# Where the slots lie in SBUF: twelve slots longer by 128 bytes, or three longer by 512

## The chip, the core and the metric

The kernel runs on one core of one Trainium2 chip. The metric is the device time of one launch in microseconds (us). Engines are named as in the profile: PE (TensorE, the matmuls), PEld (its weight loads), DVE (VectorE), ACT (ScalarE), POOL (GpSimd) and SP (SyncE, which issues the DMAs).

## The reference

A decoder block on x of 2048 x 1024 in float32. x is RMS-normed and multiplied by a 1024 x 7680 matrix; the product is cut into a GLU pair, a convolution gate, q, k, v, an attention gate and two merge gates. One branch is a causal depthwise convolution of 31 taps, layer norm, SiLU, gate and a 1024 x 1024 product; the other is attention over a window of 128 with rotary positions and a sink per head (16 query heads, 4 key heads of 64), gate and a 1024 x 1024 product.

```python
glu_in, conv_gate, q, k, v, attn_gate, merge_logits = split(rmsnorm(x, norm_g) @ w_in)
c = silu(layernorm(depthwise_conv(a * sigmoid(b))))        # glu_in = a, b
y_conv = (c * silu(conv_gate)) @ w_conv_out
y_attn = (attention(rope(q), rope(k), v, sinks) * silu(attn_gate)) @ w_attn_out
x = x + (sigmoid(m_conv) * y_conv + sigmoid(m_attn) * y_attn) @ w_out
return rmsnorm(x, final_norm_g)
```

## The kernel before, in words

The 2048 rows are worked in two sweeps of T = 1024, each sweep in two halves of 512 columns. Every large product is made in split precision: each operand is a high part and a remainder, and each block of 128 x 128 x 512 takes three matmuls, high x high, high x remainder, remainder x high (L280). `project` (L267) makes one item: for each half, 8 steps of the inner dimension with 3 matmuls, so 24 matmuls into one PSUM bank, and 48 for both halves. A sweep has 60 items that read the normed input hT (16 for the GLU, 12 for q, k and v, 32 for the gates), then 8 of the attention output (`mm_ya`, moving tiles aT), 8 of the convolution output (`mm_yc`, moving tiles uT) and the last product (L885), which is 16 blocks of 24 with the tiles wo moving and the merged activations mT as weights. Between the matmuls of the items lie those of the attention (from L554: scores `sc` L572 of 256 columns, transposes `tpp` L602, the product with v `ov` L622) and other transposes (`tpf` L361, `tpx` L327, `tpv` L502). The order on PE is written out by hand by the class `Line`, which has planned durations; it depends on no address. DVE carries the convolution (L396).

The weights of an item come through the pool `stage`: raw, high and remainder, 4 buffers of 2048 bytes a partition each, every one holding four weight matrices of 512 bytes a partition. Everything else that is large lives in 43 slots (L75 to L90): 16 named H, 16 A, 8 C and 3 X. A slot holds 1024 floats, 4096 bytes a partition; a matmul's moving operand is either half of it (high part or remainder, 2048 bytes). Slots listed in `WIDE` (all C, a14, a15, h14, h15) are 1056 floats, 4224 bytes, because a GLU tile has 30 more columns ahead of it (L415); GLU tiles only ever use c6, c7 and a14 (L379).

A pool's tiles lie one after another in the order in which their names are first used. The tiles of `const` end at byte 9024 of a partition, the slots follow, then `stage` at 186688 and `work` at 211264. Byte 9024 is 17 x 512 + 320. Since a plain slot is 8 x 512 bytes and a wide one 8 x 512 + 128, the place of a tile within 512 bytes (its remainder, below) changes behind each wide slot. Worked out from the order of use:

| tiles | remainder mod 512 |
|---|---|
| all weight buffers of `stage` | 320 |
| A0 to A5, A7 to A12, H0 to H7, C0, C6, C7 | 320 |
| H8 to H14, C1, A14 | 448 |
| H15, C2, C4 | 64 |
| A6, A13, A15, X0 to X2, C3, C5 | 192 |
| the identity for transposes (`const`) | 128 |

By address, H0 to H7 and the A tiles but A6, A13, A14 and A15 start below 87000, C0 to C3 from 90944 to 103616, H8 to H15 from 112064 to 140864, and the weights lie above 194880.

The moving tiles by item: in the first sweep hT and uT are H0 to H7 for half 0 and H8 to H15 for half 1, aT is A0 to A7 and A8 to A15. In the second, hT and uT are H8 to H15 and then A0 to A7, aT is H0 to H7 and A8 to A15. mT lies where aT lay, wo in C0 to C7 (L846). The v tiles vt are in the first four A (H in the second sweep), vd in X0 to X2 and A15; probabilities pt and pc in A7 to A10 (H7, A8 to A10 in the second sweep).

Of the kernel before, what the change touches and what calls it, by code (L numbers as in the profile page):

```python
# [12 lines left out]
F32 = mybir.dt.float32  # L13
# [6 lines left out]
P = 128  # L20
# [3 lines left out]
T = 1024  # L24
# [4 lines left out]
HALO = TAPS - 1  # L29
# [24 lines left out]
def hybrid_block(ctx: ExitStack, tc: tile.TileContext, x, par_d, w_in, w_conv, sinks, w_attn, w_out,  # L54
# [4 lines left out]
    const = ctx.enter_context(tc.tile_pool(name="const", bufs=1))  # L59
# [16 lines left out]
    A = [f"a{i}" for i in range(16)]  # L76
    C = [f"c{i}" for i in range(8)]
    X = [f"x{i}" for i in range(3)]
    WIDE = set(C) | {"a14", "a15", "h14", "h15"}

    def slot(tag, shape, dt, name):
        n = int(np.prod(shape[1:]))
        full = HALO + T + 2 if tag in WIDE else 1024
        t = slots.tile([P, full], dt, tag=tag, name=name)
        v = t[:, 0:n]
        if len(shape) == 3:
            v = v.rearrange("p (a b) -> p a b", b=shape[2])
        elif len(shape) == 4:
            v = v.rearrange("p (a b c) -> p a b c", b=shape[2], c=shape[3])
        return v  # L90
# [11 lines left out]
    def load_first(half):  # L102
        xs = []
        for j in range(4):
            r0 = (4 * half + j) * P
            xs.append(slot(A[7 * half + j], [P, D], F32, f"xf{half}_{j}"))
            nc.sync.dma_start(out=xs[-1], in_=x2[r0:r0 + P, :])
        return xs
# [4 lines left out]
    ident_r = const.tile([P, P], F32R, name="ident_r")  # L113
    ident = f(ident_r)
    ident_0 = slot(A[4], [P, P], F32, "ident_0")
    make_identity(nc, ident_0)
    dve.tensor_copy(out=ident_r, in_=ident_0)
    ones_0 = slot(A[5], [P, P], F32, "ones_0")
    dve.memset(ones_0, 1.0 / D)
    ones = const.tile([P, P], F32R, name="ones")  # L120
# [39 lines left out]

    d_a = dram.tile([NSWEEP * KC, P, 2, T], F32, name="d_a")
    v_halo = const.tile([P, NKV, 2, HD], F32R, name="v_halo")
    v_last = const.tile([P, 2, P], F32, name="v_last")
    dve.memset(v_last, 0.0)


# [798 lines left out]
```

## Time and profile before

| | |
|---|---|
| median of 3 runs | 2053.18 us (2053.03 to 2053.26) |
| the profiled execution, its own time | 2053.2 us |
| its span, first to last instruction | 2051.5 us |
| granted TensorE clock | 0.999 |
| busy PE, DVE, ACT, POOL | 99%, 65%, 50%, 20% of the span |
| DMA, mean share of 16 engines | 53.3%, 173 GB/s |

So 1.7 us lie outside the span. A matmul's recorded duration covers its way through the array and overlaps the next one's, and its end is modelled; what a matmul costs in a stream is the step from its start to the next one's start. The chain view (work that ended last, in order of time) gives a piece as start, length and count: length by count is the mean step. The timeline gives starts.

### The profile page before, as it was taken

How to read it: one execution, taken by the hardware profiler on the slowest of the kernel's cores; microseconds unless marked ns; L12 is line 12 of the kernel's file. 1: busy time of each engine (PE TensorE's matmuls, PEld its weight loads, DVE VectorE, ACT ScalarE, POOL GpSimd, SP SyncE). 2: the span in 40 equal slices, each digit the busy share in tenths (PEclk: the TensorE clock that was granted, in tenths of full speed). 3: DMA queues.
4: the chain of work that ended last, by engine and by line, in shares of the span. 5: the costliest groups of instructions: out<-in, count | busy, mean ns of one | idle time of the engine just before them, and what ended most of it. 6: DMA issues, size and time to landing. Idle time of an engine off the chain costs nothing.

```text
span 2051.5 us, 27562 instructions
## 1 busy us (share of the span) xinstructions
PE 2031.3 (99%) x9256; PEld 1669.1 (81%) x9256; DVE 1327.4 (65%) x1965; ACT 1027.8 (50%) x2313; POOL 403.4 (20%) x336
## 2 busy tenths in 40 slices
PE   7999999999999999999999999999999999999998
PEld 6888888888888888888888888888888888888886
DVE  4968769988994355123668678689888924441323
ACT  6312477777777463123433125767677764621222
POOL 2335332333323223241001120111011100001200
PEclk9999999999999999999999999999999999999999
DMA  7445655555566757444344555555555577564422
GB/s 249 144 144 167 208 170 160 166 168 172 161 188 212 252 174 244 143 157 169 131 144 138 164 178 188 160 175 174 173 156 171 179 222 257 172 228 138 153 110 82
DMA packets 265821, 355.91 MB, mean 173 GB/s; under 512 B 28112, under 2 KB 126544, under 8 KB 265680
## 3 DMA queue, kind: packets, MB, share of 16 engines
q1 hardware_dynamic: 265680, 354.16, 53.3%
q8 instruction: 73, 1.20, 0.2%
q14 instruction: 68, 0.56, 0.1%
HBM read 234.51 MB, written 119.54 MB: 173 GB/s over the span
## 4 chain that ended last, share of the span: by engine, by line
PE 96%; DVE 2%; DMA 1%; issue 0%; SPq 0%; POOL 0%; ACT 0%; DVEq 0%; POOLq 0%
PE mm_cg L281 9%; PE o L885 9%; PE mm_ma L281 9%; PE mm_ga L281 9%; PE mm_mc L281 9%; PE mm_yc L281 9%; PE mm_ya L281 9%; PE mm_gb L281 8%; PE mm_ag L281 7%; PE mm_q_a L281 4%; PE mm_q_b L281 4%; PE sc L572 3%; PE ov L622 3%; PE mm_v L281 2%; DVE acc L396 2%; PE tpp L602 1%
## 5 line engine op out<-in xcount | busy, mean ns | idle before, releaser
L396 DVE SCALAR_TENSOR_TENSOR acc<-glu,par,acc 128x1024 f32<-128x1024 f32 x464 | 596.3, 1285 | 6.2
L885 PE MATMUL o<-wo,mT 128*128 128x512 f32 x768 | 181.3, 395 | 0.0
L885 PEld LDWEIGHTS o<-wo,mT 128*128 128x128 f32 x768 | 143.2, 188 | 32.0
L281 PE MATMUL mm_cg<-hT,whi_cg 128*128 128x512 f32 x512 | 161.1, 396 | 0.0
L281 PE MATMUL mm_ga<-hT,whi_ga 128*128 128x512 f32 x512 | 160.9, 395 | 0.2 <-ACT whi_ga L253 0.2
L281 PE MATMUL mm_ma<-hT,whi_ma 128*128 128x512 f32 x512 | 161.0, 396 | 0.0
L281 PE MATMUL mm_ag<-hT,whi_ag 128*128 128x512 f32 x512 | 160.8, 395 | 0.0
L281 PE MATMUL mm_gb<-hT,whi_gb 128*128 128x512 f32 x512 | 160.7, 395 | 0.0
L281 PE MATMUL mm_mc<-hT,whi_mc 128*128 128x512 f32 x512 | 159.7, 393 | 0.0
L281 PE MATMUL mm_yc<-uT,whi_yc 128*128 128x512 f32 x512 | 159.5, 393 | 0.0
L281 PE MATMUL mm_ya<-aT,whi_ya 128*128 128x512 f32 x512 | 158.7, 391 | 0.0
L613 POOL TENSOR_SCALAR_AFFINE_SELECT pc<-pt 128x1024 fp32r<-128x1024 f32 x60 | 65.6, 1094 | 428.7 <-DVE pt L242 428.6
L281 PEld LDWEIGHTS mm_yc<-uT,whi_yc 128*128 128x128 f32 x512 | 96.2, 188 | 21.8
L281 PEld LDWEIGHTS mm_mc<-hT,whi_mc 128*128 128x128 f32 x512 | 96.1, 188 | 21.7
L281 PEld LDWEIGHTS mm_ya<-aT,whi_ya 128*128 128x128 f32 x512 | 96.1, 188 | 20.9
L281 PEld LDWEIGHTS mm_ga<-hT,whi_ga 128*128 128x128 f32 x512 | 94.6, 188 | 20.4 <-ACT whi_ga L253 0.6
L281 PEld LDWEIGHTS mm_gb<-hT,whi_gb 128*128 128x128 f32 x512 | 94.7, 188 | 19.9
L281 PEld LDWEIGHTS mm_ag<-hT,whi_ag 128*128 128x128 f32 x512 | 94.3, 188 | 19.4
L281 PEld LDWEIGHTS mm_cg<-hT,whi_cg 128*128 128x128 f32 x512 | 94.2, 188 | 19.5
L281 PEld LDWEIGHTS mm_ma<-hT,whi_ma 128*128 128x128 f32 x512 | 94.2, 188 | 19.3
L592 ACT ACTIVATE ss<-ss,st 128x128 f32<-128x128 f32 x256 | 99.7, 391 | 11.2 <-DVE st L587 10.7
L281 PE MATMUL mm_ga<-hT,wlo_ga 128*128 128x512 f32 x256 | 100.8, 394 | 0.7 <-POOL wlo_ga L242 0.7
(364 smaller groups left out, 4259.3 us busy)
## 6 DMA issues: line engine op xcount, KB each, us to landing
qk<-d_q SPq DMA_DIRECT2D x256, 64.0 KB, 2.2
d_a<-ss SPq DMA_DIRECT2D x128, 128.0 KB, 1.9
aT<-d_a SPq DMA_DIRECT2D x32, 512.0 KB, 5.5
qk<-d_k SPq DMA_DIRECT2D x240, 64.0 KB, 2.0
raw_gb<-in_w_in_dram SPq DMA_DIRECT2D x34, 256.0 KB, 3.2
raw_ga<-in_w_in_dram SPq DMA_DIRECT2D x34, 256.0 KB, 3.3
raw_ag<-in_w_in_dram SPq DMA_DIRECT2D x32, 256.0 KB, 3.7
d_ag<-ag SPq DMA_DIRECT2D x32, 256.0 KB, 2.2
```

What stands on the lines that cost most here:

```text
L281: pe.matmul(out=ps, lhsT=a, rhs=b, start=(k == 0 and i == 0), stop=(k == KC - 1 and i == 2))
L396: dve.scalar_tensor_tensor(out=to, in0=glu[c][:, j:j + T], scalar=tap(c, j), in1=acc[c], op0=ALU.mult, op1=ALU.add)
L572: pe.matmul(out=o, lhsT=q[:, h, :], rhs=r, start=(j == 0), stop=(j == 1))
L592: act.activation(out=sb[:, h, :], in_=sb[:, h, :], func=AF.Exp, scale=SCALE, bias=ngm[:, h:h + 1], accum_out=den[:, h:h + 1])
L602: pe.transpose(out=tpp[:, h, :], in_=sb[:, h, :], identity=ident)
L613: pool.affine_select(out=pc, in_=f(pt), pattern=[[0, 2], [0, GQ], [1, P]], compare_op=ALU.is_ge, fill=0.0, base=0, channel_multiplier=-1)
L622: pe.matmul(out=ov, lhsT=vv, rhs=pp[:, i % 2], start=(i == 0), stop=(i == nm - 1))
L885: pe.matmul(out=ps, lhsT=a[:, c0:c0 + P], rhs=r, start=(k == 0 and i == 0), stop=(k == KC - 1 and i == 2))
```

## The change

```diff
-    WIDE = set(C) | {"a14", "a15", "h14", "h15"}
+    WIDE = {"c6", "c7", "a14"}
...
-        full = HALO + T + 2 if tag in WIDE else 1024
+        full = 1024 + P if tag in WIDE else 1024
...
-    v_last = const.tile([P, 2, P], F32, name="v_last")
+    v_last = const.tile([P, 2 * P + 48], F32, name="v_last")[:, 0:2 * P].rearrange("p (a b) -> p a b", b=P)
```

Twelve slots were 128 bytes longer than the rest; now three are, by 512. Both add up to 1536 bytes, so the slots take as much as before. `v_last` is the last tile of `const` and grows by 48 floats, 192 bytes, of which nothing is used: the slots start at 9216 = 18 x 512, `stage` at 186880 = 365 x 512. With slots of 8 x 512 or 9 x 512 bytes and buffers of 4 x 512, every slot, every weight buffer and every weight matrix in it has the remainder 0. The identity keeps its 128. The tiles of 512 floats in `work`, which hold no operand of the large products, go from 384 to 64. No instruction is added, removed or moved, and no shape changes.

## The prediction

> **What bounds the kernel now.** The page comes first: who is busy, and what the chain that ended last is made of.
>
> ```profile
> span 2051.5 us, 27562 instructions
> PE 2031.3 (99%) x9256; PEld 1669.1 (81%) x9256; DVE 1327.4 (65%) x1965; ACT 1027.8 (50%) x2313; POOL 403.4 (20%) x336
> PE 96%; DVE 2%; DMA 1%; issue 0%; SPq 0%; POOL 0%; ACT 0%; DVEq 0%; POOLq 0%
> ```
>
> PE is the chain. The view of waits, for PE alone, says how much of the span it stood still:
>
> ```profile
> PE tpf L361 <- DVE ident_r L117: 8.4, 1, 8.4
> PE tpf L361 <- DVE xf L354: 2.4, 2, 1.5
> PE sc L572 <- DVE pt L242: 1.0, 1, 1.0
> ```
>
> The two longest are the start, before there is anything to multiply; the third is the longest wait after it, 1.0 us. So the time is the sum of PE's steps, and the question is whether a step depends on where its operands lie. The chain view of two neighbouring blocks of one `mm_yc` item of the first sweep, in which nothing is put between the matmuls, answers it:
>
> ```profile
> 874.48 5.45 PE mm_yc L281 x24
> ...
> 879.93 5.59 PE mm_yc L281 x24
> ```
>
> Same instruction, same shape, same weights (remainder 320); the first block's moving tiles are H0 to H7 (320), the second's H8 to H15 (448, the last 64). The second takes 0.14 us longer, in each of the eight items of this stage. The timeline of the first, where the moving tile is H2 and later, and of the second:
>
> ```profile
> 875.92 0.62 PE L281 MATMUL mm_yc<-uT,whi_yc 128*128 128x512 f32 x2
> ...
> 880.00 0.62 PE L281 MATMUL mm_yc<-uT,whi_yc 128*128 128x512 f32 x2
> ...
> 885.59 0.40 PE L281 MATMUL mm_yc<-uT,whi_yc 128*128 128x512 f32 x1
> ```
>
> From 875.92 to 880.00 are 18 matmuls: 4.08 / 18 = 0.2267 us a step. I call this the settled step: moving operand and weights have the same remainder, and it holds without scatter. The first 6 of that block, still 320 by 320, took 5.45 - 4.08 = 1.37, some 0.228 each: they come right behind a block that did not match, and the stream needs a few matmuls to settle. From 880.00 to 885.59 are 24 steps of 0.2329, and these never settle.
>
> Where the two sweeps swap their tiles, the slow half swaps too (H8 to H15 are half 1 in the first sweep and half 0 in the second), so it goes with the tile and not with the half.
>
> **The change part by part.** All moving tiles and all weights of the large products get the remainder 0, so all of them match. The sum takes every step of theirs at 0.2267. No row shows a pair at remainder 0 itself. I take 0.2267, because it is the only steady value of a matching pair, and matching is what 320 by 320 and 0 by 0 share; the step is bounded above by the 0.2329 of blocks that never settle (the bound below follows where its row stands).
>
> The items and last stages, from the chain view (the first two rows are of a window of the first sweep, the others of the whole span):
>
> ```profile
> 103.14 11.03 PE mm_q_b L281 x48
> 114.16 11.04 PE mm_gb L281 x48
> ...
> 764.63 87.99 PE mm_ya L281 x384
> 852.62 88.33 PE mm_yc L281 x384
> 1069.97 11.07 PE mm_kb L281 x48
> 1127.13 11.07 PE mm_gb L281 x48
> 1171.43 11.07 PE mm_q_a L281 x48
> 1779.53 87.67 PE mm_ya L281 x384
> 1867.19 88.57 PE mm_yc L281 x384
> 1955.77 88.72 PE o L885 x384
> ```
>
> An item of 48 settled steps takes 48 x 0.2267 = 10.88. In the first sweep that saves some 0.155 (11.03 and 11.04), in the second 0.19 (11.07). With 60 such items a sweep: 9.3 + 11.4 = 20.7 us.
>
> A stage of 384 settled steps takes 87.05. That saves 0.94 and 0.62 in the two `mm_ya`, 1.28 and 1.52 in the two `mm_yc`, and 1.67 in the last product; the first sweep's last product is cut up by transposes, and I give it the same 1.67. Together 7.7 us.
>
> The attention has small work between the items. One attention step in the chain view:
>
> ```profile
> 570.60 0.44 PE tpp L602 x4
> 571.03 2.78 PE mm_ma L281 x12
> 573.81 0.94 PE ov L622 x4
> ...
> 575.44 0.95 PE sc L572 x8
> ```
>
> `ov` takes 0.94 for four 512-column steps, of which two have weights at 192; settled it is 0.91, so 0.03 in each of 60 steps (the first step of a key head in the first sweep has no vd): 2.0 us. The scores read q and k from one tile, so they match before and after, and I take no gain; if they came down from 0.119 a step to half of 0.2267, it would be 0.0055 x 8 x 64 = 2.8 us.
>
> Against this stands what goes on unsettling the stream: the identity of the transposes keeps its remainder 128, and the scores are short. The timeline behind one group of scores, in 320 by 320 tiles:
>
> ```profile
> 659.16 1.11 PE L572 MATMUL sc<-qk 128*128 128x256 f32 x8
> 660.11 0.63 PE L281 MATMUL mm_ma<-hT,whi_ma 128*128 128x512 f32 x2
> ...
> 661.49 0.62 PE L281 MATMUL mm_ma<-hT,whi_ma 128*128 128x512 f32 x2
> 661.94 0.39 PE L281 MATMUL mm_ma<-hT,wlo_ma 128*128 128x512 f32 x1
> ```
>
> Six steps from 660.11 to 661.49 take 1.38, against 1.36 settled: 0.02. (The next two, 661.49 to 661.94, take 0.225 each, the shortest pair that these rows show: the bound below for a step at remainder 0.) Behind transposes the chain above has 12 steps in 2.78, against 2.72 settled: 0.06, high rather than low, since half of them read tiles at 448. The counts:
>
> ```profile
> L572 PE MATMUL sc<-qk 128*128 128x256 f32 x480 | 67.1, 282 | 1.0 <-DVE pt L242 1.0
> L602 PE MATMUL tpp<-ident_r,ss 128*128 128x128 f32 x256 | 38.3, 272 | 0.0
> L327 PE MATMUL tpx<-ident_r,x 128*128 128x128 f32 x64 | 9.6, 272 | 0.0
> L502 PE MATMUL tpv<-ident_r,vs 128*128 128x128 f32 x32 | 4.8, 272 | 0.0
> ```
>
> That is 352 / 4 = 88 groups of transposes and some 64 of scores, 88 x 0.06 + 64 x 0.02 = 6.6 us in a stream that matches everywhere. Half of them fall into matching blocks today and cost this already; the other half is new, 3.3 us.
>
> Sum: 20.7 + 7.7 + 2.0 - 3.3 = 27.1 us. The profiled execution took 2053.2 (the median is 2053.18), so about 2026.
>
> The rest I cost at nothing. The start, 8.4 + 2.4 us of waits, hangs on the identity and on x, no large product. A faster PE asks for its inputs sooner, and DVE is the engine with least room, in the table of windows (busy us of PE, PEld, DVE, ACT and POOL in 50 us):
>
> ```profile
> 300.00:350.00 50.00, 50.00 (x239) 41.46 (x238) 48.59 (x66) 35.53 (x89) 13.08 (x12) 1.00 0.51 162
> ```
>
> If that were the bound wherever attention and convolution share DVE in the first sweep, some 300 us, the 1.3% won there, 4 us, would come back as waits of `sc` on `pt`. I leave it to the range. The forecast's own range is 2020 (no new unsettling, and the gain on the scores: 20.7 + 7.7 + 2.0 + 2.8 = 33) to 2039 (a match helps only where nothing is put between: 7.7 and some 20 items a sweep at 0.17, so 14.5).
>
> **The rivals.** First, that the pair at remainder 0 doesn't settle, because 320 is a good place and equality not the reason. Then every step costs 0.2329: items take 11.18, so 60 x 0.145 + 60 x 0.11 = 15.3 more, and the six stages 89.4, so 6.6 more: 22 us slower, 2075. It turns from gain to loss where fewer than about four steps in ten settle, (232.9 - 230.3) / (232.9 - 226.7), with 11.05 / 48 = 0.2303 as the mean now. For it speaks one place in the last product, where a tile at 192 meets weights at 192:
>
> ```profile
> 2036.85 0.70 PE o L885 x3
> ```
>
> 0.233 a step. But these three stand behind tiles at 64 and 192 over weights at 320, and three are too few to settle. Against it: at 320 the tiles of A and of H settle alike, wherever in the lower half of the slots they lie, and with all eight buffers of weights. Chance 0.11.
>
> Second, no change, 2053: the slow tiles are slow for another reason that the change leaves, such as lying high in SBUF, where H8 to H15 remain. For it: H8 to H15 lie above 112000. Against it: in the last product half of the moving tiles, C0 to C3, start below 104000, and at 88.72 / 384 = 0.231 it is the slowest of the tail stages; and the weights lie at the top always. Chance 0.06. The Trainium skill, "TensorE: Matmul & The Clock Gate", step-by-step section of Part 2, would come out here too: it gives PE two independent read ports, so that loading the next weights takes nothing from the running matmul. The two blocks of one item above, 5.45 against 5.59, speak against that as the whole story.
>
> Third, more than forecast: at 512-byte boundaries the settled step is shorter than at 320, down to the 0.225 above. Another 8064 x 0.0017 = 14 us, 2012. Chance 0.05. The Trainium skill, on the same page under "Wait — 56ns, not 53.3ns?", measures 215.7 ns for a warm stream of 512 columns; by that figure the time would be near 1938 as an estimate, and no step of this trace that lasts comes near it.
>
> **How the numbers follow.** The forecast has 0.78. The range leaves out the slower rival (0.11), the deeper gain and a little of the forecast's tails, and takes in no change: 2016 to 2054; the forecast alone has 2020 to 2039. Two parts in a thousand, 4 us, is what a measurement of this kernel can tell from no change: faster 0.78 + 0.05 = 0.83, same 0.06, slower 0.11.
>
> **What would show it.** In the chain view both blocks of an item take 5.44, an undisturbed item 10.88 to 10.9, `mm_ya`, `mm_yc` and the last product 87.0 to 87.3 each. DVE, ACT and DMA groups keep their durations, and PE's waits stay those of the start. If items take 11.18, the first rival holds; if one half of an item still takes 0.14 more than the other, the second; blocks under 5.43, the third. If blocks take 5.44 but the span is not 20 us shorter, the difference must stand as waits of PE on DVE between 300 and 620.

## The result, and the profile after

The changed kernel takes 2028.53 us (2028.24 to 2029.28, 4 runs) against 2053.18 (2053.03 to 2053.26, 4 runs): 24.65 us less, a ratio of 0.9881 with a 95% interval of 0.9863 to 0.9898. The profiled execution took 2029.28, its span is 2027.6.

The first lines of the page, after:

```profile
span 2027.6 us, 27562 instructions
PE 2006.5 (99%) x9256; PEld 1667.3 (82%) x9256; DVE 1324.5 (65%) x1965; ACT 1026.0 (51%) x2313; POOL 403.3 (20%) x336
PE 96%; DVE 2%; DMA 1%; issue 0%; SPq 0%; POOL 0%; ACT 0%; DVEq 0%; POOLq 0%
```

The instructions are the same, and so is the make-up of the chain. PE's busy time fell by 24.8 us, DVE's by 2.9, ACT's by 1.8, POOL's by 0.1. The chain view says where; the columns are start, length, what, and how many:

```profile
57.17 10.88 PE mm_kb L281 x48
...
102.67 10.88 PE mm_q_b L281 x48
113.56 10.88 PE mm_gb L281 x48
...
757.48 87.04 PE mm_ya L281 x384
844.52 87.04 PE mm_yc L281 x384
931.56 19.04 PE o L885 x84
...
1759.43 87.04 PE mm_ya L281 x384
1846.47 87.04 PE mm_yc L281 x384
1933.51 87.05 PE o L885 x384
```

Where before every stage had its own length (87.67 to 88.72), now each is 87.04 or 87.05, and an undisturbed item is 10.88: 0.2267 us a step, in all of them. What is left above that lies around the small work, in the same place of the first sweep that the prediction showed:

```profile
565.44 0.44 PE tpp L602 x4
565.88 2.78 PE mm_ma L281 x12
568.66 0.91 PE ov L622 x4
...
570.25 0.95 PE sc L572 x8
```

The 12 steps behind the transposes still take 2.78, `ov` came from 0.94 to 0.91, and the scores kept their 0.95. The view of waits, for PE:

```profile
PE tpf L361 <- DVE ident_r L117: 8.4, 1, 8.4
PE tpf L361 <- DVE xf L354: 2.7, 2, 1.8
PE sc L572 <- DVE pt L242: 1.3, 1, 1.3
PE tpf L361 <- DVE hT L364: 0.8, 1, 0.8
```

The same waits, the last three longer by 0.3 each; the last of them was, before:

```profile
PE tpf L361 <- DVE hT L364: 0.5, 1, 0.5
```

### The profile page after: what moved, and what is told of

Same layout as the page of the kernel before. It is cut to its first block, busy times and chain, and to the rows that moved or that the text cites. A ratio compares the mean times of both kernels' runs of the same rounds, so it can differ in the third digit from the quotient of the medians.

```text
span 2027.6 us, 27562 instructions
## 1 busy us (share of the span) xinstructions
PE 2006.5 (99%) x9256; PEld 1667.3 (82%) x9256; DVE 1324.5 (65%) x1965; ACT 1026.0 (51%) x2313; POOL 403.3 (20%) x336
## 4 chain that ended last, share of the span: by engine, by line
PE 96%; DVE 2%; DMA 1%; issue 0%; SPq 0%; POOL 0%; ACT 0%; DVEq 0%; POOLq 0%
PE mm_cg L281 9%; PE mm_ma L281 9%; PE mm_ga L281 9%; PE o L885 9%; PE mm_mc L281 9%; PE mm_yc L281 9%; PE mm_ya L281 9%; PE mm_gb L281 8%; PE mm_ag L281 7%; PE mm_q_a L281 4%; PE mm_q_b L281 4%; PE sc L572 3%; PE ov L622 3%; PE mm_v L281 2%; DVE acc L396 2%; PE tpp L602 1%
## 5 line engine op out<-in xcount | busy, mean ns | idle before, releaser
L396 DVE SCALAR_TENSOR_TENSOR acc<-glu,par,acc 128x1024 f32<-128x1024 f32 x464 | 596.0, 1285 | 6.2
L592 ACT ACTIVATE ss<-ss,st 128x128 f32<-128x128 f32 x256 | 99.7, 390 | 11.4 <-DVE st L587 10.8
```

Of the source, the lines that this page charges most:

```text
L396: dve.scalar_tensor_tensor(out=to, in0=glu[c][:, j:j + T], scalar=tap(c, j), in1=acc[c], op0=ALU.mult, op1=ALU.add)
L592: act.activation(out=sb[:, h, :], in_=sb[:, h, :], func=AF.Exp, scale=SCALE, bias=ngm[:, h:h + 1], accum_out=den[:, h:h + 1])
```

## The experiments

The theory under test: a stream of matmuls settles at 0.2267 us a step when its moving operand and its weights start at equal places within 512 bytes, wherever that is, and at no other time. The rivals: the multiple of 512 itself counts; only one of the two operands counts; or something else that moved along.

**All at 320.** The changed kernel without the 192 bytes, which is the kernel before with the new slot lengths alone.

```diff
-    v_last = const.tile([P, 2 * P + 48], F32, name="v_last")[:, 0:2 * P].rearrange("p (a b) -> p a b", b=P)
+    v_last = const.tile([P, 2 * P], F32, name="v_last")[:, 0:2 * P].rearrange("p (a b) -> p a b", b=P)
```

> The changed kernel without the 192 bytes: every slot and every weight buffer has the remainder 320 instead of 0, so all pairs are equal but none is a multiple of 512. Theory 1 (equal remainders of moving tile and weights settle the stream): 2028 to 2029 us, both blocks of an item 5.44. Rival (the multiple of 512 itself counts): back to the step that never settles, 2053 to 2075 us.

Measured: 2027.53 us (2026.86 to 2028.35, 4 runs), ratio 0.9876 (0.986 to 0.9893). The stages are 87.04 and 87.05, the items 10.88; two lines of its chain view:

```profile
1758.08 87.04 PE mm_ya L281 x384
1845.12 87.04 PE mm_yc L281 x384
```

So the multiple of 512 is not needed; the whole gain comes from the slots.

**The 192 bytes alone.** The kernel before, with the longer `v_last` only.

> The kernel before with the 192 bytes alone: the twelve slots stay wide, all remainders move by 192 together (weights at 0, A and H0 to H7 at 0, H8 to H14 at 128). Theory 1: which pairs are equal is unchanged, 2053 us. Rival (tiles at multiples of 512 gain by themselves): below 2049.

Measured: 2053.01 us, beside 2053.37 of the kernel before on the same chip. Its last product takes 88.72, as before. The two runs undo and do one half of the change each, and agree: the 192 bytes do nothing for the time.

**The weights moved away.** The slots stay at 0; the last slot is made longer, so that all weight buffers (and the tiles of `work` behind them) move by 128, 64, 32 or 256 bytes. The edit for 128 bytes, 32 floats; the others have 16, 8 and 64:

```diff
         full = 1024 + P if tag in WIDE else 1024
+        full += 32 if tag == "c5" else 0
```

> The changed kernel with the last slot 128 bytes longer: slots at 0, weight buffers at 128; the last product, whose weights lie in slots, stays equal. Theory 1: no block of the items settles, 5.59 each, so 120 items x 0.30 = 36 more and the four stages of 384 at 89.4, 9.5 more: 2070 to 2074 us. Rival (the moving tiles' places alone count): no change, 2028 us.

> The same with 64 bytes. Theory 1, strictly mod 512: as with 128 bytes, 2070 to 2074 us. If what must be equal is the remainder by 64 bytes or less, which all tiles of the kernel before shared, 2028 us; but then the kernel before had no unequal pairs, so this is not expected.

> Slots at 0, weight buffers at 32. Theory 1, strictly equal: 2062 to 2072 us. If only the 64-byte piece in which an operand starts must be the same: 2028 us.

> Slots at 0, weight buffers at 256. Theory 1 (mod 512): no item settles, as with 64 and 128 bytes: 2062 to 2072 us. If equality mod 256 is enough: 2028 us.

Measured, one run each: 2064.42 us at 128, 2070.44 at 64, 2069.33 at 32, and 2029.27 at 256. In the chain view the same item of the first sweep, at 128 and then at 256:

```profile
102.88 11.20 PE mm_q_b L282 x48
```

```profile
102.32 10.88 PE mm_q_b L282 x48
```

And the stages of 384, first at 128 and then at 64:

```profile
769.48 89.23 PE mm_ya L282 x384
858.71 89.24 PE mm_yc L282 x384
```

```profile
772.13 89.60 PE mm_ya L282 x384
861.73 89.60 PE mm_yc L282 x384
```

89.60 / 384 = 0.2333 and 89.23 / 384 = 0.2324: the two sizes of a stream that never settles (at 32 the stages take 89.60 too, and undisturbed items take 11.20, 0.2333 a step, at 32 and 64, and all but three of them at 128). These runs show that weights and moving tiles count together: the moving tiles lie at 0 in all four. Each run has its own control: the last product takes its weights from slots, which did not move, and still takes 87.06 to 87.08 at 128, 64 and 32. The runs also correct the theory. Of the offsets tried, 32, 64 and 128 bytes unsettle the stream and 256 does not, so equality is needed modulo 256 bytes, not 512: at 256 everything is as in the changed kernel. 32 bytes off is as bad as 64, so it is not enough to start in the same 64-byte piece.

At 128 the time was 6 us under the range that was expected. Summing the steps between matmul starts over the traces of this run and the changed kernel: the four stages took 8.8 us more, against 9.5 expected, and the items 27.7 more, against 36. Most of the miss is in the items: the expectation took all of them as settled in the changed kernel, where those around the small work are not.

**Control: `work` alone.** The runs before moved the tiles of `work` too. Here only they move, by 128 bytes.

```diff
-        csum = work.tile([P, T], F32, tag="ln0", name=f"csum{s}", bufs=1)
+        csum = work.tile([P, T + 32], F32, tag="ln0", name=f"csum{s}", bufs=1)[:, 0:T]
```

(The two other tiles of that name likewise.)

> Control for the runs that moved the weights, where the tiles of work behind them moved too: slots and weights at 0, only the tiles of work 128 bytes further. Theory 1: 2028 us, since none is an operand of the large products. If the places of what ACT and DVE write count: part of the 36 us between the changed kernel and the weights at 128.

Measured: 2029.95 us, with stages of 87.04; its span, 2028.2 us, is 0.6 us longer than that of the changed kernel. The tiles of `work` play no part in the step.

**The identity at 0.** Does its remainder of 128 unsettle the stream behind transposes?

```diff
+    const.tile([P, 96], F32, name="pad0")
     ident_r = const.tile([P, P], F32R, name="ident_r")
```

(And 128 bytes more behind `v_last`, so that the slots start at a multiple of 512 again.)

> The changed kernel with the identity for the transposes at remainder 0 too (384 bytes ahead of it, 128 fewer behind). If it is the identity's remainder that unsettles the stream behind a transpose: up to 88 x 0.06 = 5 us less, 2023 to 2026. If it is the transpose's short shape: 2028 to 2029 us.

Measured: 2027.61 us (2027.19 to 2028.03, 4 runs), ratio 0.9877 (0.9862 to 0.9892): no difference from the changed kernel that its interval can tell; beside this run the kernel before was 0.6 us faster as well (2052.62). The place that was shown after the transposes, in this run:

```profile
564.05 0.44 PE tpp L603 x4
564.49 2.75 PE mm_ma L282 x12
```

2.75 instead of 2.78, and 2.72 would be settled: over 64 such places 2 us at most. So at most a small part of the unsettling behind a transpose goes with the identity's address. The transpose's shape is what is left of the two; no run changed it.

**Narrow weight loads.** What are the 13.3 ns by which a settled step exceeds 512 columns at the clock of up to 2.4 GHz that the Trainium skill gives for TensorE ("TensorE: Matmul & The Clock Gate", the table under its title)? They are an estimate, 226.7 - 512 / 2.4; the traces show the granted share of the clock, 0.999, and not the clock itself. If they are a share for the weight load beside it, a narrower load should shorten the step.

```diff
-                        pe.matmul(out=ps, lhsT=a, rhs=b, start=(k == 0 and i == 0),
+                        m = {"ya": 64, "yc": 32}.get(name[:2], P) if i == 1 else P
+                        pe.matmul(out=ps[0:m], lhsT=a[:, 0:m], rhs=b, start=(k == 0 and i == 0),
```

> The changed kernel, in which the matmul high x remainder takes only 64 weight columns in the mm_ya items and 32 in the mm_yc items, so that part of those products is left out; one weight load in three is narrower, the moving columns stay 512. If the 13.3 ns of the settled step beyond 512 columns at 2.4 GHz belong to the weight load beside it, in proportion: an mm_ya stage of 384 takes 86.2 (2.2 ns a step less) and an mm_yc stage 85.8 (3.3 less), against 87.04. If they belong to the moving stream itself: 87.04 in both.

> The same with the weights at 64, where no item settles and both stages take 89.6 of 384 steps of 233.3 ns. If what unsettles is the meeting of the two streams, a narrower load meets less: mm_ya 88.3, mm_yc 87.7 (all 20 ns beyond 512 columns in proportion to the load). If the extra is the moving stream's own: 89.6 in both.

Measured, one run each: 2034.20 us with equal operands, 2067.74 with the weights at 64 (the edit for 64 bytes on top). Both kernels leave out part of the products. Neither expectation came true in the first of the two. Its chain view:

```profile
756.65 88.23 PE mm_ya L282 x384
844.88 88.74 PE mm_yc L282 x384
```

Narrower loads made the step longer, 229.8 and 231.1 ns: the stream no longer settles. With the weights at 64 the stages are 89.60 and 88.75, so there `mm_ya` didn't change and `mm_yc` is a little shorter; neither 88.3 and 87.7 nor 89.6 in both, the two expectations. The narrow loads were shorter in fact; the groups of PEld in the first of the two runs, whose second figure behind the bar is the mean in ns:

```profile
L282 PEld LDWEIGHTS mm_ya<-aT,whi_ya 128*128 128x128 f32 x256 | 48.0, 188 | 11.0
...
L282 PEld LDWEIGHTS mm_ya<-aT,whi_ya 128*64 128x64 f32 x256 | 34.4, 134 | 10.9
L282 PEld LDWEIGHTS mm_yc<-uT,whi_yc 128*32 128x32 f32 x256 | 27.6, 108 | 11.2
```

One load in three was narrow, so the irregular order could be the reason. The last run makes all loads of a block narrow but two, and leaves out most of these products:

```diff
-                        m = {"ya": 64, "yc": 32}.get(name[:2], P) if i == 1 else P
+                        m = {"ya": 64, "yc": 32}.get(name[:2], P) if 0 < 3 * k + i < 23 else P
```

> The changed kernel, in which all matmuls of a block but its first and last take only 64 weight columns in the mm_ya items and 32 in the mm_yc items, so most of those products is left out; the loads are narrow but regular. If one narrow load in three unsettled the stream because it broke the regularity, and the settled step holds a share for the load: mm_ya under 87.04 (84.7 if in proportion, 22 of 24 steps at 220 ns), mm_yc lower still (83.5, at 216.7). If regular narrow loads settle at the same step: 87.04 in both. If narrow loads never settle, whatever their order: 88 to 90 in both.

Measured: 2034.91 us, one run. In the chain view:

```profile
757.11 88.22 PE mm_ya L282 x384
845.33 88.87 PE mm_yc L282 x384
```

With narrow loads the stream didn't settle in either order. So the width of the weights acts on the step, though moving columns and addresses are the same; and the 13.3 ns are not a cost in proportion to the load. A narrow load comes with a matmul that writes fewer partitions (`ps[0:m]`), and no run parts the two, so it is not shown which of them does it. That the two reads of PE, moving operand and weights, meet in SBUF and fall into step when load and stream start alike is an account that fits the runs on addresses. With the further assumption that a narrower load meets less, it forecast 88.3 and 87.7 with the weights at 64, where 89.60 and 88.75 came. No run shows the meeting itself, so it stays argued.

## Why the prediction was right, point by point

**The step.** Right, and shown: the settled 0.2267 holds for every stage and every undisturbed item, at 0 as at 320. That equality counts and not the place was the assumption on which the first rival hung; the run with all at 320 and those with the weights moved settle it. The three slow matmuls with tile and weights both at 192, which spoke for that rival, stood behind pairs that did not match and were too few to settle; no run has a longer stream at 192.

**Equal modulo what.** The prediction took 512, and it is 256. So H15, C2 and C4, at 64, did match weights at 320 before. Each gives three matmuls behind a tile that did not match, too few to settle; this is argued from the order of the tiles. Nothing in the sum hung on it, since it took the stages as measured.

**The second rival,** no change, falls with the result: H8 to H15 still lie high in SBUF and now take the same step as the rest. The Trainium skill gives PE two independent read ports, so that loading the next weights takes nothing from the running matmul ("TensorE: Matmul & The Clock Gate", step-by-step section of Part 2). The traces differ: moving the weights' address, with the moving tiles left where they were, changes the running stream's step by up to 6.7 ns, 0.2333 against 0.2267. Whether that arises at the ports or behind them, no run shows.

**The third rival,** a shorter step at multiples of 512, is refuted by the 87.04 that stages take with all at 0 and with all at 320.

**The sum.** 27.1 us were forecast, and the two profiled executions differ by 23.9. The starts of the stages in the chain views split it. One more row of before, the first piece of the first sweep's last product, serves for this:

```profile
940.95 19.44 PE o L885 x84
```

| stretch | before | after | saved | forecast |
|---|---|---|---|---|
| start to first `mm_ya` | 764.63 | 757.48 | 7.15 | 9.3 + 1.0 - 1.65 = 8.65 |
| `mm_ya` and `mm_yc`, first sweep | 176.32 | 174.08 | 2.24 | 2.22 |
| last product of the first sweep, items of the second | 838.58 | 827.87 | 10.71 | 1.67 + 11.4 + 1.0 - 1.65 = 12.4 |
| `mm_ya` and `mm_yc`, second sweep | 176.24 | 174.08 | 2.16 | 2.14 |
| last product | 88.72 | 87.05 | 1.67 | 1.67 |

The stages without small work came out to a few hundredths. The miss is in the other two stretches, 1.5 and 1.7 us, and is made of small terms. Summing the steps between matmul starts over the traces: the first sweep's last product saved 1.19 and not 1.67, because transposes cut it up; `ov` saved 1.5 and not 2.0; the scores, costed at nothing, took 0.7 us more (60.3 to 61.0 without the one wait), and no run shows why; the waits of PE rose by 0.9, as the view of waits shows. The items that lie between the attention's steps saved 8.9, against a forecast of 36 x 0.155 + 36 x 0.19 - 3.3 = 9.1. Without that price the forecast for them would be 12.4, so the new unsettling cost 3.5 there. The prediction's 3.3 was meant for the whole kernel; its prices for the 64 groups of transposes and 64 of scores of the attention alone give 0.5 x (64 x 0.06 + 64 x 0.02) = 2.6. So the term was right in kind and somewhat low.

**DVE as the next bound.** It was left to the range, and it stayed small. In the table of windows, after:

```profile
300.00:350.00 50.00, 48.74 (x238) 40.70 (x237) 49.43 (x68) 36.13 (x85) 13.23 (x13) 1.00 0.53 170
```

DVE is as good as full there, 49.43 of 50, and PE lost 1.26 us in this window to the one wait of the scores on `pt`. Before, the same wait stood just behind the window's end, ahead of the score that starts at 351.97, so most of this is no new loss: the wait is 0.3 us longer. That a still faster PE would pay here next is an inference from DVE's share; no run shows it.

## What to carry to other kernels

Where PE is the chain and never waits, compare its steps between neighbouring blocks that differ in nothing but their buffers: a difference that goes with the buffer points at its address, and a run that moves only that buffer settles it. For matmuls like these (float32r in the kernel, 512 moving columns, 128 weight columns, a weight load for each), let moving tiles and weights start at the same place modulo 256 bytes; a slot that is longer by a few columns should be rounded up to that, and it costs nothing when few slots need to be long. The new slot lengths alone did it here, 2027.53 us without the 192 bytes.

## What the runs showed of the hardware

- A stream of such matmuls settles at 226.7 ns a step if moving operand and weights are equal modulo 256 bytes. Off by 32, 64 or 128 bytes it doesn't, and takes 233.3, 233.3 and 232.4 ns in `mm_ya` and `mm_yc`.
- After something that unsettles it, it takes a few matmuls to settle again. Averaged by place from the matmul starts of the changed kernel, the steps are back at 226.6 to 227.3 ns from the twelfth on behind the transposes of the attention and from the sixth on behind eight scores.
- With matmuls of 64 or 32 weight columns, one in three, it doesn't settle at equal addresses either: 229.8 and 231.1 ns. Their loads were shorter, 134 and 108 ns against 188, and the step was longer, which neither account expected.
- DVE's convolution kept its 1285 ns an instruction through the change.
